# Two transformer layers on one core: who loads first, and which engine does the small casts, sums and block additions

## The chip, the core and the metric

One core of a Trainium2 chip runs the whole program. Its engines work side by side, each through its own queue of instructions in a fixed order: TensorE (PE in the profile; PEld is its weight load), VectorE (DVE), ScalarE (ACT), GpSimd (POOL) and SyncE (SP). An instruction that has to wait holds up all that stand behind it on its engine. The metric is the device time of one execution in microseconds; the kernel before takes 326.74 us, the median of 3 runs (326.48 to 327.2).

## The reference

Two layers over 256 tokens of 1024 features. Everything is float32; the kernel keeps float32 accuracy by splitting each operand of a big product in two.

```python
def even_layer(x, norm_g, w_in, b_f, gn_g, w_out):
    h = rms_norm(x, norm_g)
    q_f, k_f, v_f, f_l, q_r, k_r, v_r, z = jnp.split(h @ w_in, EVEN_SPLITS, axis=-1)
    o_f = fox_attention(q_f, k_f, v_f, f_l + b_f)        # 8 heads, forget gates
    o_r = retention(q_r, k_r, v_r) * gn_g                # 8 heads, group norm
    return x + (concatenate([o_f, o_r]) * silu(z)) @ w_out

def odd_layer(x, ...):
    h = rms_norm(x, norm_g)
    q, kc, vc, ks, vs, kw, vw, gl, z = jnp.split(h @ w_in, ODD_SPLITS, axis=-1)
    k_cmp = silu((blocks of 32 tokens of kc + pe_k) @ wk1) @ wk2      # the same for v_cmp
    o = gated sum of attention to compressed blocks, selected blocks, and a window
    return x + (o * silu(z)) @ w_out

out = rms_norm(odd_layer(even_layer(x)), final_g)
```

## The kernel before, in words

**The stream of big products.** The weights of both layers come as 38 chunks of up to 280 columns (1 MB each). `Feed.load` fetches a chunk into one of three stage buffers `st` (line 148), `Feed.split` cuts it by quarters into `wh` (a copy at the precision of the product, line 95 on ScalarE, line 97 on VectorE) and `wl` (the rest in bf16, line 102 on VectorE), and a chunk feeds two units of 8 steps. A step is three products on TensorE: high by high (lines 194, 214), low by high (195, 215), bf16 by `wl` (196, 216). The next chunk is loaded once a stage buffer is free. The other operand is split the same way, k = 0 to 7 in slices of 128 features: `h` (x0h, x1h, y0h, y1h), `l` (x0l, x1l ..., line 119 or 102) and `b`, the bf16 copy of `h` (x0b, x1b, y0b, y1b; line 99, on GpSimd).

**The first loads.** xT (the input, in four pieces of 256 KB, two slices of k each) and chunk 0 (in_w0v, four pieces of 264 KB) are issued in turn by SyncE, all in one queue, with gv (the factors of the norms) ahead and chunk 1 (two halves), the biases, the constants and chunk 2 behind. Of the slices x0h, ScalarE makes k = 0, 1, 2, 4, 5, 6 and VectorE k = 3 and 7. While the loads are on their way TensorE runs 24 products of zeros (`warm`).

**The norms.** Layer 0 squares xT on ScalarE and adds the eight squares up in a tree of three additions (`sq`, then `acc_n`): the first on VectorE, the others on GpSimd. pc_n and pn_n (lines 257, 248) sum over the partitions on TensorE, and r_n, R_n (243, 244) are the factors; the first values (line 306, 308) leave PSUM with them. The other two norms add one square after the other into `acc_n` on GpSimd (line 240 calls line 102), the last square of the final norm aside.

**The compressed blocks.** After the out projection of layer 0 (products pp_o, additions `xT` at line 381, then x1h, x1l, x1b and the square of each m), `build` takes keys and values kc, vc and writes `ab`: for each of the 4 pairs of kv and u one multiply (line 427) and 8 additions of pe on VectorE. The products `ph` (line 707) take all of ab; TensorE reaches the first of them between two units of pp_ks.

**The order.** The text of the kernel is laid out by a scheduler that fixes the queue of each engine when the program is built; it weighs the loads and operations by its own estimates. So an edit in one place can move instructions in another. The end is the multiply of x2 by R_n in five pieces on VectorE and GpSimd (lines 876 to 880), each followed by its store.

Of the kernel before, what the change touches and what calls it, by code (L numbers as in the profile page):

```python
# [10 lines left out]
F32 = mybir.dt.float32  # L11
# [19 lines left out]
NEARLY = _C["T0"][0]   # columns that layer 0 needs  # L31
# [14 lines left out]
LEAD = 22          # steps by which a chunk of weights is split ahead of its first product  # L46
# engine of each small operation: A scalar, V vector, G gpsimd
E = dict(whi="AAAA", wlo="VVVV", xhi="AAAAAAAA", x0hi="AAAVAAAV", w0hi="AAAV", xb="G", sq="A", acc="G", yhi="A", ylo="G", yb="G", sz="G",
         q2h="AA", q2l="GG", a0="A", a1="V", ac="V", norm="GGGG", pn="G", kh="AA", kl="VV", ab="VVVV", pT="A", cs="GG", tree="VGG", xg="AAAAAAAA")
FIN = (("V", 0, 1), ("G", 1, 1), ("V", 2, 2), ("G", 4, 1), ("V", 5, 3))  # L50
# [3 lines left out]
def trunk_kernel(ctx: ExitStack, tc: tile.TileContext, a: dict):  # L54
# [19 lines left out]

    A.preload_act_table_set("natural_log_exp_and_others")
# [52 lines left out]
    # A chunk is up to 280 columns of a weight matrix: loaded, split into wh (f32r) + wl (bf16), and used by  # L128
    # two units of 8 steps. run(n) issues the next n steps, with the splits and loads that are due.
    class Feed:  # L130
# [11 lines left out]
        def load(s, parts=1, between=None):  # L142
# [4 lines left out]
            for i in range(parts):  # L147
                nc.sync.dma_start(c["st"][:, q * i:q * i + q, :n], c["ap"][:, q * i:q * i + q, :])
                if between:
                    between(i)  # L150
            s.loaded += 1

        def split(s):
            """the next quarter of a chunk"""
# [27 lines left out]
    def mtile(col, xs, kind, name, done):  # L182
        """128 output features as partitions, all tokens; done(psum) after the last step."""
# [18 lines left out]
    def vtile(tt, x, kind, name, done):  # L202
        """128 tokens as partitions, the chunk's columns free."""
# [18 lines left out]
    class Norm:  # L222
        """sum of squares over features -> rsqrt(mean + eps), as [P, S] and as columns."""
# [55 lines left out]
    # ================= layer 0: the stream =================  # L279
# [722 lines left out]
```

## Time and profile before

| | |
|---|---|
| median of 3 runs | 326.74 us |
| span of the profiled execution, first to last instruction | 324.8 us |
| TensorE busy | 307.5 us, 95% of the span |
| VectorE busy | 228.9 us, 70% |
| ScalarE busy | 202.7 us, 62% |
| GpSimd busy | 126.3 us, 39% |
| mean granted TensorE clock | 0.987 of full |
| read from HBM | 48.24 MB |

The runs are timed around the span, and their median stands 1.9 us above it. TensorE is busy for nearly the whole span, so its gaps and its clock are what one looks for first; the shares of the other engines say little, since each is nearly full in some stretches and idle in others.

### The profile page before, as it was taken

How to read it: one execution, taken by the hardware profiler on the slowest of the kernel's cores; microseconds unless marked ns; L12 is line 12 of the kernel's file. 1: busy time of each engine (PE TensorE's matmuls, PEld its weight loads, DVE VectorE, ACT ScalarE, POOL GpSimd, SP SyncE). 2: the span in 40 equal slices, each digit the busy share in tenths (PEclk: the TensorE clock that was granted, in tenths of full speed). 3: DMA queues.
4: the chain of work that ended last, by engine and by line, in shares of the span. 5: the costliest groups of instructions: out<-in, count | busy, mean ns of one | idle time of the engine just before them, and what ended most of it. 6: DMA issues, size and time to landing. Idle time of an engine off the chain costs nothing.

```text
span 324.8 us, 6784 instructions
## 1 busy us (share of the span) xinstructions
PE 307.5 (95%) x2478; PEld 256.4 (79%) x2478; DVE 228.9 (70%) x686; ACT 202.7 (62%) x547; POOL 126.3 (39%) x202
## 2 busy tenths in 40 slices
PE   6879999999999999999987999999999999999990
PEld 4668888888888887888875767898988898888870
DVE  2978964665656656189998856798978798882433
ACT  4749545666645556287622647598988898881461
POOL 2450011541522133375200001267779777973152
PEclk9999999999999999999997999999999999999997
DMA  6995897664155334407717892325421442100003
GB/s 180 363 308 197 264 390 257 227 226 142 59 171 178 132 108 153 129 2 219 244 69 240 281 314 89 127 67 195 131 64 69 133 129 76 56 2 0 3 0 129
DMA packets 43138, 49.72 MB, mean 153 GB/s; under 512 B 1633, under 2 KB 39777, under 8 KB 42849
## 3 DMA queue, kind: packets, MB, share of 16 engines
q1 hardware_dynamic: 42816, 49.03, 45.9%
q8 instruction: 19, 0.31, 0.4%
q10 hardware_dynamic: 288, 0.26, 0.2%
q14 instruction: 15, 0.11, 0.1%
HBM read 48.24 MB, written 1.05 MB: 152 GB/s over the span
## 4 chain that ended last, share of the span: by engine, by line
PE 73%; DVE 16%; ACT 3%; DMA 2%; POOL 2%; issue 1%; SPq 1%; DVEq 0%; ACTq 0%
DVE wl L102 6%; PE pp_q L194 5%; PE pp_z L196 4%; PE pp_q L196 4%; PE pp_z L194 4%; PE pp_z L195 4%; PE pp_q L195 4%; PE pp_o L196 4%; PE po L838 4%; PE pp_o L194 4%; PE pp_o L195 3%; PE ph L707 3%; DVE ab L102 3%; PE pp_k L194 3%; PE pp_k L196 2%; PE pp_k L195 2%
## 5 line engine op out<-in xcount | busy, mean ns | idle before, releaser
L102 DVE TENSOR_TENSOR wl<-st,wh 128x512 bf16<-128x512 f32 (+2 forms) x152 | 108.2, 740 | 13.8 <-ACT wh L95 12.0
L95 ACT ACTIVATE wh<-st 128x512 fp32r<-128x512 f32 (+2 forms) x151 | 87.6, 621 | 43.1 <-PE pp_o L195 8.5
L196 PEld LDWEIGHTS <-wl 128*128 128x128 bf16 x512 | 49.0, 96 | 22.5 <-issue 0.2
L108 POOL TENSOR_SCALAR p<-p,st 128x128 f32<-128x128 f32 (+1 forms) x80 | 42.7, 551 | 51.3 <-DVE st L598 31.9
L782 ACT ACTIVATE p<-ns,st 128x128 f32<-128x128 f32 (+1 forms) x64 | 28.4, 444 | 7.7 <-DVE st L770 6.2
L102 POOL TENSOR_TENSOR q<-q,q 64x256 fp32r<-64x256 f32 x16 | 12.1, 754 | 45.9 <-ACT q L95 44.8
L214 PE MATMUL pp_v<-wh,x0h 128*128 128x256 f32 (+1 forms) x64 | 23.4, 368 | 1.4 <-ACT wh L95 1.4
L194 PE MATMUL pp_o<-y0h,wh 128*128 128x256 f32 x64 | 23.3, 366 | 0.4 <-DVE xT L381 0.4
L194 PE MATMUL pp_q<-x0h,wh 128*128 128x256 f32 x64 | 23.5, 368 | 0.0
L194 PE MATMUL pp_k<-x0h,wh 128*128 128x256 f32 x64 | 23.2, 365 | 0.0
L194 PE MATMUL pp_z<-x0h,wh 128*128 128x256 f32 x64 | 23.2, 365 | 0.0
L194 PE MATMUL pp_o<-y1h,wh 128*128 128x256 f32 x64 | 23.1, 363 | 0.0
L194 PE MATMUL pp_q<-x1h,wh 128*128 128x256 f32 x64 | 22.7, 356 | 0.0
L194 PE MATMUL pp_z<-x1h,wh 128*128 128x256 f32 x64 | 22.6, 355 | 0.0
L770 DVE CUSTOM_DVE_ANT_0 ns<-s,cst 128x128 f32<-128x128 f32 (+1 forms) x64 | 20.1, 350 | 0.0
L216 PE MATMUL pp_v<-wl,x0b 128*128 128x256 bf16 (+1 forms) x64 | 17.9, 283 | 1.1 <-DVE wl L102 1.0
L196 PE MATMUL pp_z<-x0b,wl 128*128 128x256 bf16 x64 | 18.1, 283 | 0.0
L196 PE MATMUL pp_q<-x0b,wl 128*128 128x256 bf16 x64 | 18.1, 283 | 0.0
L196 PE MATMUL pp_o<-y0b,wl 128*128 128x256 bf16 x64 | 18.1, 283 | 0.0
L196 PE MATMUL pp_o<-y1b,wl 128*128 128x256 bf16 x64 | 18.1, 283 | 0.0
L196 PE MATMUL pp_k<-x0b,wl 128*128 128x256 bf16 x64 | 18.1, 283 | 0.0
L196 PE MATMUL pp_q<-x1b,wl 128*128 128x256 bf16 x64 | 18.1, 283 | 0.0
(322 smaller groups left out, 1000.9 us busy)
## 6 DMA issues: line engine op xcount, KB each, us to landing
st<-in_w0c_dram SPq DMA_DIRECT2D x13, 1024.0 KB, 5.8
st<-in_w1c_dram SPq DMA_DIRECT2D x12, 1024.0 KB, 5.6
w<-in_wkv_dram SPq DMA_DIRECT2D x8, 512.0 KB, 4.8
st<-in_w0o_dram SPq DMA_DIRECT2D x4, 1024.0 KB, 5.7
st<-in_w1o_dram SPq DMA_DIRECT2D x4, 1024.0 KB, 5.6
st<-in_w1v_dram SPq DMA_DIRECT2D x2, 1120.0 KB, 5.0
st<-in_w0c_dram SPq DMA_DIRECT2D x4, 512.0 KB, 8.9
dec<-in_dec_dram SPq DMA_DIRECT2D x2, 768.0 KB, 7.7
```

Of the source, the lines that this page charges most:

```text
L95: A.activation(o, x, AF.Copy)
L102: (V if e == "V" else G).tensor_tensor(o, x, y, op=op)
L108: (V if e == "V" else G).tensor_scalar(o, x, c, 1.0, op0=OP.mult, op1=OP.mult)
L194: T.matmul(p, wh[:, k, cs], x.h[:, k], start=(k == 0), stop=False)
L195: T.matmul(p, wh[:, k, cs], x.l[:, k], start=False, stop=False)
L196: T.matmul(p, wl[:, k, cs], x.b[:, k], start=False, stop=(k == KT - 1))
L214: T.matmul(p, x.h[:, k, ts], wh[:, k, :n], start=(k == 0), stop=False)
L216: T.matmul(p, x.b[:, k, ts], wl[:, k, :n], start=False, stop=(k == KT - 1))
L707: T.matmul(ph[64 * kv:64 * kv + 64, :256], ab[:, kv, 2 * qr + j].rearrange("p g c -> p (g c)"), w1[qr][:, kv, j], start=(qr == 0 and j == ...
L770: V.tensor_tensor_reduce(out=out, in0=pp[:, lo:lo + n], in1=C(tab, lo, lo + n), scale=-slope, scalar=3e38, op0=OP.add, op1=OP.min, accum_o ...
L782: A.activation(p[:, d:d + n], ns[:, d:d + n], AF.Exp, scale=-1.0, bias=st[:, qt, br, 0:1], accum_out=st[:, qt, br, 1:2])
L838: T.matmul(po[64 * j:64 * j + 64, 256 - n:256], vs[:, kt, vc:vc + 64], m[:, br * n:br * n + n], start=False, stop=(br == 1 and kt == 1))
```

## The change

- gv is issued by GpSimd's queue, xT by SyncE's, chunk 0 by ScalarE's, ahead of its table load. Chunks 1 and 2 follow on SyncE.
- The bf16 copies `b` (x0b, y0b, x1b, y1b: 32 casts), the sums `acc_n` of the norms (13 additions) and the tree of layer 0 (2 additions) run on VectorE.
- `build` writes ab in 4 additions of 64 x 240 elements per call where it took 8 of 64 x 120.
- The last multiply is three pieces (3, 3 and 2 slices), all on VectorE.

```diff
-E = dict(... xb="G", sq="A", acc="G", yhi="A", ylo="G", yb="G", sz="G",
-         ... cs="GG", tree="VGG", xg="AAAAAAAA")
-FIN = (("V", 0, 1), ("G", 1, 1), ("V", 2, 2), ("G", 4, 1), ("V", 5, 3))
+E = dict(... xb="V", sq="A", acc="V", yhi="A", ylo="G", yb="V", sz="G",
+         ... cs="GG", tree="VVV", xg="AAAAAAAA")
+FIN = (("V", 0, 3), ("V", 3, 3), ("V", 6, 2))
...
-        kc4 = kc.rearrange("p (b j r) -> p b j r", j=8, r=2)
         for gi in range(2):
             gr = slice(64 * gi, 64 * gi + 64)
             for par in range(2):
-                for jh in range(2):
-                    binary(E["ab"][2 * gi + par],
-                           ab[64 * par:64 * par + 64, kv, 8 * jh:8 * jh + 8, 2 * u + gi, 0:15],
-                           kc4[gr, jh:jh + 15, :, par].rearrange("p c j -> p j c"),
-                           pe[gr, kv, par, 8 * jh:8 * jh + 8].unsqueeze(2).to_broadcast([64, 8, 15]), OP.add)
+                o = ab[64 * par:64 * par + 64, kv, :, 2 * u + gi, 0:15].rearrange("p (h j) c -> p h j c", h=2)
+                x = bass.AP(kc.tensor, kc[gr, par:par + 1].offset, [list(kc[gr].ap[0]), [16, 2], [2, 8], [16, 15]])
+                y = pe[gr, kv, par].rearrange("p (h j) -> p h j", h=2).unsqueeze(3).to_broadcast([64, 2, 8, 15])
+                binary(E["ab"][2 * gi + par], o, x, y, OP.add)
...
-    nc.sync.dma_start(gv, a["gv"])
...
-    nc.sync.dma_start(xT[:, 0:2], a["xT"][:, 0:2])
-    def more(i):
-        if i < 3:
-            nc.sync.dma_start(xT[:, 2 * i + 2:2 * i + 4], a["xT"][:, 2 * i + 2:2 * i + 4])
-    feed.load(4, more)
+    nc.gpsimd.dma_start(gv, a["gv"])
+    for i in range(4):
+        nc.sync.dma_start(xT[:, 2 * i:2 * i + 2], a["xT"][:, 2 * i:2 * i + 2])
+    feed.load(4, nc.scalar)
+    A.preload_act_table_set("natural_log_exp_and_others")
     feed.load(2)
```

**First place: VectorE's queue at the start.** x0h, x0l and x0b are slices of 128 x 256; what an instruction waits for stands in brackets. Before (DMAHW1, 3, 5 and 7 are the four pieces of xT, 2 and 4 pieces of chunk 0):

```order
L119 SCALAR_TENSOR_TENSOR x0l<-xT,gv,x0h 128x256 [waits DMAHW1_49,DMAHW0_49,Activation_49]
L119 SCALAR_TENSOR_TENSOR x0l<-xT,gv,x0h 128x256 [waits Activation_49]
L108 TENSOR_SCALAR x0h<-xT,gv 128x256 [waits DMAHW3_49]
L102 TENSOR_TENSOR wl_170<-st_147,wh_169 128x2x264 [waits DMAHW2_49,Activation_49]
L119 SCALAR_TENSOR_TENSOR x0l<-xT,gv,x0h 128x256 [waits Activation_49]
L119 SCALAR_TENSOR_TENSOR x0l<-xT,gv,x0h 128x256 [waits DVE_49]
L102 TENSOR_TENSOR wl_170<-st_147,wh_169 128x2x264 [waits DMAHW4_49,Activation_49]
```

The same place now, where DMAHW1, 2, 4 and 6 are the four pieces of xT in their order, DMASW0 is gv, and DMAHW0 is the first piece of chunk 0:

```order
L106 TENSOR_SCALAR x0h<-xT,gv 128x256 [waits DMAHW2_49,DMASW0_49]
L117 SCALAR_TENSOR_TENSOR x0l<-xT,gv,x0h 128x256 [waits DVE_49]
L95 CAST x0b<-x0h 128x256
L106 TENSOR_SCALAR x0h<-xT,gv 128x256 [waits DMAHW6_49]
L117 SCALAR_TENSOR_TENSOR x0l<-xT,gv,x0h 128x256 [waits DMAHW1_49,Activation_49]
L95 CAST x0b<-x0h 128x256
L117 SCALAR_TENSOR_TENSOR x0l<-xT,gv,x0h 128x256 [waits Activation_49]
L95 CAST x0b<-x0h 128x256
L100 TENSOR_TENSOR wl_170<-st_149,wh_169 128x2x264 [waits DMAHW0_49,Activation_49]
```

VectorE's own two slices (k = 3, from the second piece, and k = 7, from the last) have moved ahead of x0l of k = 0, and each x0l is followed by its cast.

**Second place: VectorE's queue at the end of layer 0's out projection and in `build`.** Before, around the additions of m = 4 and 5 and the first blocks:

```order
L381 TENSOR_TENSOR xT<-pp_o_4_1825,xT 128x256 [waits PE_49]
L102 TENSOR_TENSOR wl_1776<-st_1580,wh_1775 128x2x256 [waits Activation_49] x2
L119 SCALAR_TENSOR_TENSOR x1l<-xT,gv,x1h 128x256 [waits Activation_49]
L102 TENSOR_TENSOR wl_1871<-st_1677,wh_1870 128x2x256 [waits DMAHW1_49,Activation_49]
L102 TENSOR_TENSOR wl_1871<-st_1677,wh_1870 128x2x256 [waits Activation_49]
L381 TENSOR_TENSOR xT<-pp_o_5_1863,xT 128x256 [waits PE_49]
...
L427 TENSOR_TENSOR kc_2055<-pp_kc_1981,R_n_2045 128x256 [waits Activation_49]
L427 TENSOR_TENSOR kc_2065<-pp_kc_2009,R_n_2045 128x256
L102 TENSOR_TENSOR ab<-kc_2055,pe 64x8x15 [waits DVE_49]
L102 TENSOR_TENSOR ab<-kc_2055,pe 64x8x15 x7
```

The same rows now:

```order
L377 TENSOR_TENSOR xT<-pp_o_4_1825,xT 128x256 [waits PE_49]
L100 TENSOR_TENSOR wl_1871<-st_1677,wh_1870 128x2x256 [waits DMAHW0_49]
L100 TENSOR_TENSOR wl_1871<-st_1677,wh_1870 128x2x256
L117 SCALAR_TENSOR_TENSOR x1l<-xT,gv,x1h 128x256 [waits Activation_49]
L95 CAST x1b<-x1h 128x256
L100 TENSOR_TENSOR acc_n_96<-acc_n_96,sq_n_1860 128x256 [waits Activation_49]
L377 TENSOR_TENSOR xT<-pp_o_5_1863,xT 128x256 [waits PE_49]
...
L423 TENSOR_TENSOR kc_2055<-pp_kc_1981,R_n_2045 128x256 [waits Activation_49]
L423 TENSOR_TENSOR kc_2061<-pp_kc_2009,R_n_2045 128x256
L100 TENSOR_TENSOR ab<-kc_2055,pe 64x16x15 [waits DVE_49]
L100 TENSOR_TENSOR ab<-kc_2055,pe 64x16x15 x3
```

Between two additions of xT there are now a cast and a sum more, and a block takes 4 additions in place of 8.

## Rows read from the trace of the kernel before

**Rows 1.** Waits of TensorE: us in total, times, longest.

```profile
PE ph L707 <- DVE ab L102: 3.1, 1, 3.1
PE pc_n L257 <- POOL acc_n L102: 1.9, 1, 1.9
PE pp_v L214 <- ACT wh L95: 1.4, 1, 1.4
...
PE pp_o L194 <- DVE xT L381: 0.4, 1, 0.4
```

**Rows 2.** Windows: us; busy PE, PEld, DVE, ACT, POOL; PEclk, DMA share, GB/s.

```profile
19.50:20.50 1.00, 0.00 (x0) 0.00 (x0) 1.00 (x2) 0.06 (x1) 0.92 (x2) 1.00 1.03 312
...
139.00:158.00 19.00, 18.56 (x153) 16.17 (x153) 19.00 (x31) 14.55 (x32) 12.01 (x15) 1.00 0.45 140
...
173.00:202.00 29.00, 29.00 (x217) 20.82 (x213) 20.67 (x45) 17.24 (x41) 0.52 (x1) 0.94 0.72 243
```

**Rows 3.** Chain that ended last, first 21 us: start, us, what.

```profile
4.36 0.85 SPq L539
5.26 7.23 DMA st<-in_w0v_dram
...
15.57 4.07 POOL sq L102
...
20.81 0.61 PE pc_n L257 x4
```

**Rows 4.** Tile xT in the first 20 us: ns, and time to landing.

```profile
L119 DVE SCALAR_TENSOR_TENSOR x0l<-xT,gv,x0h x8: 476/612/620, 6.2 to 13.3; 128x256 fp32r<-128x256 f32 x8
...
DMA to landing us min/median/max: 4.4/5.5/6.6
```

**Rows 5.** Timeline of VectorE at the start: start us, us, what.

```profile
12.86 0.87 DVE L119 SCALAR_TENSOR_TENSOR x0l<-xT,gv,x0h 128x256 fp32r<-128x256 f32 x2
...
14.27 1.22 DVE L102 TENSOR_TENSOR sq<-sq 128x1024 f32<-128x1024 f32 x1
...
24.32 0.57 DVE L308 SCALAR_TENSOR_TENSOR fl<-pp_v,r_n,bias 128x8 f32<-128x8 f32 x2
```

**Rows 6.** Timeline of TensorE: two steps of chunk 2, and ph.

```profile
24.61 0.37 PE L214 MATMUL pp_v<-wh,x0h 128*128 128x256 f32 x1
...
24.98 0.36 PE L214 MATMUL pp_v<-wh,x0h 128*128 128x256 f32 x1
...
172.59 1.78 PE L707 MATMUL ph<-w,ab 128*64 128x256 f32 x10 [3.08 <-DVE ab L102]
```

**Rows 7.** Timeline of VectorE, out projection of layer 0 to the blocks.

```profile
138.88 1.15 DVE L381 TENSOR_TENSOR xT<-pp_o,xT 128x256 f32<-128x256 f32 x3 [4.55 <-PE pp_o L196]
...
147.39 1.28 DVE L102 TENSOR_TENSOR wl<-st,wh 128x512 bf16<-128x512 f32 x2
...
150.66 1.22 DVE L102 TENSOR_TENSOR wl<-st,wh 128x512 bf16<-128x512 f32 x1
...
160.05 0.74 DVE L427 TENSOR_TENSOR kc<-pp_kc,R_n 128x256 f32<-128x256 f32 x2
160.72 5.13 DVE L102 TENSOR_TENSOR ab<-kc,pe 64x120 f32<-64x120 f32 x16
```

**Rows 8.** Groups of VectorE by shape: count, busy us, mean ns.

```profile
L102 DVE TENSOR_TENSOR ab<-kc,pe 64x120 f32<-64x120 f32 x32 | 9.9, 350 | 0.2
L102 DVE TENSOR_TENSOR KL<-kf,KH 64x256 fp32r<-64x256 f32 x16 | 6.7, 418 | 0.5 <-ACT KH L95 0.3
...
L102 DVE TENSOR_TENSOR KL<-kcf,KH 64x16 fp32r<-64x16 f32 x8 | 1.4, 172 | 0.2
...
L336 DVE CAST sel<-cst 104x1024 fp32r<-104x1024 f32 x1 | 0.7, 682 | 0.0
```

**Rows 9.** Timeline of the last multiply.

```profile
318.28 2.95 DVE L102 TENSOR_TENSOR xT<-xT,R_n 128x256 f32<-128x256 f32 x3 [2.25 <-ACT R_n L244]
318.32 2.09 POOL L102 TENSOR_TENSOR xT<-xT,R_n 128x256 f32<-128x256 f32 x2 [3.80 <-ACT R_n L244]
```

More of the change, by code (lines that the diff above doesn't have):

```diff
@@ L46 @@
 LEAD = 22
-E = dict(whi="AAAA", wlo="VVVV", xhi="AAAAAAAA", x0hi="AAAVAAAV", w0hi="AAAV", xb="G", sq="A", acc="G", yhi="A", ylo="G", yb="G", sz="G",
-         q2h="AA", q2l="GG", a0="A", a1="V", ac="V", norm="GGGG", pn="G", kh="AA", kl="VV", ab="VVVV", pT="A", cs="GG", tree="VGG", xg="AAAAAAAA")
-FIN = (("V", 0, 1), ("G", 1, 1), ("V", 2, 2), ("G", 4, 1), ("V", 5, 3))
+E = dict(whi="AAAA", wlo="VVVV", xhi="AAAAAAAA", x0hi="AAAVAAAV", w0hi="AAAV", xb="V", sq="A", acc="V", yhi="A", ylo="G", yb="V", sz="G",
+         q2h="AA", q2l="GG", a0="A", a1="V", ac="V", norm="GGGG", pn="G", kh="AA", kl="VV", ab="VVVV", pT="A", cs="GG", tree="VVV", xg="AAAAAAAA")
+FIN = (("V", 0, 3), ("V", 3, 3), ("V", 6, 2))
 @with_exitstack
@@ L73, in bank @@
         return pool.tile([P, 512], F32, tag=tag, name=name)
-    A.preload_act_table_set("natural_log_exp_and_others")
     xT = cp.tile([P, KT, S], F32, name="xT")
@@ L140, in chunk, with load @@
                 s.steps.append(lambda f=fns[i], k=k: f(k))
-        def load(s, parts=1, between=None):
+        def load(s, parts=1, queue=nc.sync):
             c = s.chunks[s.loaded]
@@ L147, in load @@
             for i in range(parts):
-                nc.sync.dma_start(c["st"][:, q * i:q * i + q, :n], c["ap"][:, q * i:q * i + q, :])
-                if between:
-                    between(i)
+                queue.dma_start(c["st"][:, q * i:q * i + q, :n], c["ap"][:, q * i:q * i + q, :])
             s.loaded += 1
```

## The prediction

> **What bounds the kernel now.** I read first who waits for whom on TensorE, since it is busy for 95% of the span: each gap in it is time, and work on another engine counts only where it makes or closes one. There are three gaps worth naming [rows 1]: 3.1 us before ph, which waits for the blocks ab; 1.9 us before pc_n, for the sum of squares acc_n; 1.4 us before the first product. The windows [rows 2] add the clock. In the stretch from 173 to 202 us, which begins with the gap before ph, the mean granted clock is 0.94: 6% of 29 us at full speed is 1.7 us of TensorE's work lost, since the clock stood at its lower level, 1.2 GHz, for some 3.5 us. So the gap before ph costs 3.1 + 1.7 = 4.8 us. The wait for acc_n, 1.9 us long, left the clock at 1.00 [rows 2]: here 1.9 us of idleness did no harm to it and 3.1 us did.
>
> The timeline of VectorE [rows 7] says why ph waits. From 138.88 us VectorE goes without a pause: additions, splits and low parts until 160.05, then the blocks until ab is whole and ph goes on at 172.59 [rows 6]. In the window from 139 to 158 it is busy 19.00 of 19 us [rows 2], with TensorE at 18.56. So here, and only here, VectorE sets the pace; from 173 us to the end of the last product TensorE does, and work given to VectorE there lies under it.
>
> **The change part by part.** *VectorE from 138.88 to 160.05, 21.17 us.* Here stand 18 splits wl, 8 additions xT, 8 low parts x1l. Beside a silent GpSimd two wl take 1.28 us, some 0.60 apiece with the small overlap; one alongside a GpSimd operation takes 1.22 [rows 7]. Of x0l two take 0.87, 0.435 apiece, against a median of 0.61 for one [rows 5, 4]. Three additions take 1.15, some 0.35 apiece with overlap [rows 7]. Undisturbed: 18 x 0.60 + 8 x 0.35 + 8 x 0.435 = 17.1 us. So about 4 us of the 21.17 is VectorE and GpSimd slowing each other, and with the casts and sums gone from GpSimd it goes. What comes is 8 casts x1b and 7 sums. No row has this cast; the nearest is sel, 1024 elements in 0.682 us [rows 8], so 256 lie between a quarter of that, 0.17, and the 0.42 of a two-operand operation of 256 [rows 8]; I take 0.25, near the sel row, which is a copy too: 2.0 us (1.4 to 3.4). The sums are like KL, 0.418, or 0.35 with overlap: 2.45. Together 17.1 + 2.0 + 2.45 = 21.55 us, 0.4 more than now (-0.2 to +1.8): here the extra work is paid for by the peace. The blocks begin at about 160.45.
>
> *The blocks.* 16 additions of 120 elements take 5.13 us, 0.32 apiece [rows 7]; two of them are now one of 240. KL gives 172 ns for 16 elements and 418 for 256 [rows 8], that is 156 ns plus 1.025 per element. By this line 120 elements would take 279, yet ab shows 350 [rows 8]: 71 more, for its short strided runs. If that grows with the runs, 240 elements take 156 + 246 + 142 = 544 ns, 0.51 with the overlap; if it is paid once, 0.44 with it. No row shows the new form: the ends are 0.40 (the plain line) and 0.64 (nothing saved). I take 0.50, next to what growing runs give. Then from 160.45: two kc 0.67, 16 x 0.50 = 8.0, two more kc 0.7, two wl 1.2: ab is whole at 171.0 (169.4 to 173.2).
>
> *The gap before ph.* TensorE comes to it at 172.59 - 3.08 = 169.5 [rows 6]; I take 169.7, since some units of pp_o now wait a little longer for the later additions xT. The gap falls to 1.3 us, under the 1.9 that left the clock alone. ph starts 1.6 us sooner and the 1.7 of the clock are kept: -3.3 us. At the ends: ab at 169.4 closes the gap, -2.7 - 1.7 = -4.4; ab at 173.2 leaves it and the slow clock, +0.6.
>
> *The start.* In the order of VectorE's queue its x0h of k = 7 stands before x0l of k = 0, and it waits for the last piece of xT. TensorE's second product needs x0l of k = 0, so beyond its first product TensorE stands until then; queued behind the wait on VectorE are all the low parts and casts of x0 but k = 3's, and the wl of chunks 0 to 2. Before, the last piece was issued at 4.36 [rows 3] and landed 6.6 us later [rows 4], at 10.96; the last of chunk 0 landed at 5.26 + 7.23 = 12.5 [rows 3]. Now all eight are in flight from two queues, half a microsecond sooner. If the last of xT is as the last of eight, it lands at 12.0; if xT's pieces of 256 KB get ahead of the weights it may come by 8.4, 2.5 us sooner than now. I take 10.2, the middle.
>
> The Trainium skill (DMA: Bandwidth & Descriptors, "Issuing engines are not separate DMA queues") says that loads issued from several engines run on the same DMA engines and that only issue time is saved. The DMA share of 1.03 at 312 GB/s [rows 2] is of that kind: these engines are full while the loads come. By the rule alone the last of xT would land at 10.5 or later, against 10.2, and the sum would be 0.3 higher.
>
> From that landing VectorE has, in order: x0h 0.35, 7 x0l 3.05, 7 x0b 1.75, wh 0.35, and 5 wl of which the last is the last quarter of chunk 0: 3.1; that is 8.6 us. Then 3 wl, the tree's 1024 elements in 1.14 [rows 5], wl, 512 in 0.6, wl, 256 in 0.35: 5.1, and acc_n is there at 10.2 + 13.7 = 23.9, against 20.8 now [rows 3], though GpSimd's 4.07 and 1.06 us are gone. Then two wl, sel and the first fl (0.25, half the pair of 0.57 [rows 5]), 2.05 us, and chunk 2 may start, as its PSUM bank is held until fl has read it: 25.95 us. Before, chunk 2 starts at 24.61 [rows 6]. So the start loses 1.35 us (-0.45 at 8.4, +3.15 at 12.0). TensorE itself keeps up: 96 products of chunks 0 and 1 at 0.12 us, three to a step of 0.37 [rows 6], are 11.5 us, and half of them can run as VectorE feeds them. Its 4 us of idleness before may drop its clock as at ph; in the 3.5 us that this lasted there it falls behind by 1.7 us, about what it has spare (8.6 us for 50 products of 0.12, 6.0 us). gv on GpSimd's queue has no row; between nothing and the 4.4 us that a piece of xT takes [rows 4] it still comes before the slice that VectorE waits for. The table load behind four issues on ScalarE, and a decay table that is now issued ahead of chunk 3, lie under the same wait and under 5.8 us of TensorE's work per chunk.
>
> *The rest.* y0b and y1b, 16 casts, are 4 us on VectorE where TensorE sets the pace: nothing, with as their cover the slack of VectorE there; the waits for y1h that they bring hold up its queue by little (price up to 0.5 us). The last sums: nothing, VectorE idles between the last additions.
>
> *The end.* Now the three pieces on VectorE take 2.95 us beside GpSimd's 2.09 [rows 9]. By the 1024 elements in 1.22 [rows 5], undisturbed pieces of 768, 768 and 512 take 0.87 + 0.87 + 0.69 = 2.4. The last store starts 0.5 us sooner, but the first, of three slices, starts 0.5 later; I take -0.4 (-0.9 to -0.1).
>
> **Sum.** +1.35 - 3.3 - 0.4 = -2.35: the span of 324.8 becomes 322.45. The median of the runs lies 1.94 above the span (326.74), and I let that stand: 324.4 us.
>
> **The rivals.** *Slower: the new additions cost as two.* At 0.64 apiece ab is whole at 173.2, the gap is 3.5 us and the clock falls as before: 326.74 + 1.35 + 0.6 - 0.4 = 328.3. For it: the 71 ns that short runs already cost; against it: the 156 ns fixed that KL shows. It decides at the gap at which the clock falls, between 1.9 and 3.1 us; ab whole at 171.6 to 172.8, so 0.54 to 0.61 apiece. *The start is starved and the clock stays low.* TensorE gets its products by handfuls until about 19 us; if the clock is at 1.2 GHz until then, 50 products take 12 us in place of 8.6, and the start loses 3.4 more: 327.8. For it: the gap is longer than that before ph; against it: there the clock came back while TensorE worked. *The queues do what they are named for.* If the last of xT lands by 8.4 the start gains 0.45 in place of losing 1.35: 322.6. For it: eight issues need 2 us in place of 5; against it: a full DMA. *Nothing much:* the gap at ph stays at 2 us, the clock holds by half, the start loses 2.5: about 326.5.
>
> **How the numbers follow.** Forecast 50%, 323.2 to 325.9. New additions as two 13%, low clock at the start 12%, gain at the start 15%, nothing much 10%. A measurement of this kernel can tell about 0.2%, 0.65 us, from no change. Faster by more: the forecast (0.49) and the gain (0.15), 0.64. Within it: "nothing much" and a share of the two slow ones, 0.14. Slower: the rest of these, 0.22. The range, from the gain at the start to the slow cases but for their ends: 322.2 to 328.0.
>
> **What would show it.** Right: a gap before ph under 2 us and a clock of 1.00 from 173 to 202; ab at about 0.5 us each; wl at 0.6 throughout 139 to 158; TensorE idle after its first product until about 11 us, its next wait ended by x0l; chunk 2 starting near 26. Wrong: casts at 0.4 or sums at 0.7 between 139 and 158, a clock below 1.00 there or in the first 20 us, or the first low part made before 9 us.

## The result, and the profile after

The changed kernel takes 334.45 us (median of 4 runs, 333.28 to 334.76) against 326.61 us: a ratio of 1.0239 (95% interval 1.0205 to 1.0273), 2.4% slower, 7.8 us. The prediction said 324.4 us, at most 328.0. The profiled execution has a span of 333.0 us (324.8 before) and a mean granted clock of 0.972 (0.987).

Waits of TensorE after (us in total, times, longest):

```profile
PE pp_v L210 <- ACT wh L93: 4.6, 1, 4.6
PE ph L698 <- DVE ab L100: 2.9, 1, 2.9
PE po L821 <- DVE ac L816: 2.5, 7, 0.7
...
PE pp_v L211 <- DVE x0l L117: 0.6, 1, 0.6
...
PE s L750 <- POOL q L100: 0.4, 1, 0.4
```

Against [rows 1]: the wait for acc_n is gone, the one before ph is as long as it was (2.9 for 3.1), the one before the first product has grown from 1.4 to 4.6, and one is new, seven times, 2.5 us: po, the output of the sparse attention, waits for ac (the transposed attention weights of the compressed blocks, copied by VectorE out of PSUM, where the products are written).

How far the profile after lags behind the one before, at the same instruction: first product of chunk 2 +3.1 us (27.74 for 24.61), first kc +2.9, ph +2.2 (174.76 for 172.59), first po of the sparse attention +4.6 (229.38 for 224.81), its last +8.1, end of the span +8.2. So 3 us are lost at the start, one is won back on the way to ph, 2.4 go between ph and po, and 3.5 in the eight tiles of the sparse attention (a tile is two heads; its period is the time from po to the next po), where the prediction looked for nothing.

The start, on ScalarE and VectorE (start us, us, what; in brackets the idle time before and what ended it):

```profile
8.38 0.91 ACT L104 ACTIVATE x0h<-xT,gv 128x256 fp32r<-128x256 f32 x2 [3.81 <-DMA gv<-in_gv_dram]
```

```profile
8.38 0.35 DVE L106 TENSOR_SCALAR x0h<-xT,gv 128x256 fp32r<-128x256 f32 x1 [7.10 <-DMA gv<-in_gv_dram]
...
10.25 0.35 DVE L106 TENSOR_SCALAR x0h<-xT,gv 128x256 fp32r<-128x256 f32 x1 [0.79 <-DMA xT<-in_xT_dram]
```

gv, 14 KB, issued at 1.27, lets its readers go at 8.38. The last piece of xT is there at 10.25, where the prediction had 10.2. The windows after (us; busy PE, PEld, DVE, ACT, POOL; clock; DMA share, GB/s):

```profile
8.00:12.00 4.00, 1.54 (x4) 1.13 (x5) 2.79 (x9) 3.62 (x9) 0.00 (x0) 0.50 1.05 356
12.00:16.00 4.00, 3.61 (x17) 2.99 (x16) 4.00 (x12) 3.68 (x8) 0.00 (x0) 0.50 1.01 368
16.00:20.00 4.00, 4.00 (x29) 3.63 (x27) 4.00 (x10) 3.45 (x7) 0.00 (x0) 0.79 0.71 269
...
142.00:161.00 19.00, 18.63 (x154) 16.31 (x154) 18.95 (x46) 14.50 (x33) 0.00 (x0) 1.00 0.44 134
176.00:205.00 29.00, 29.00 (x216) 20.62 (x214) 18.63 (x42) 15.89 (x39) 0.00 (x0) 0.96 0.72 232
```

Having stood still from 5.3 to 9.9 us, TensorE makes its first products at 1.2 GHz. From 142 to 161 GpSimd is silent, as intended, with VectorE as full as before [rows 2].

VectorE after, in that stretch, in the blocks, and at the last multiply:

```profile
144.09 0.29 DVE L95 CAST x1b<-x1h 128x256 bf16<-128x256 f32 x1
...
144.89 0.42 DVE L100 TENSOR_TENSOR acc_n<-acc_n,sq_n 128x256 f32<-128x256 f32 x1
...
147.10 1.28 DVE L100 TENSOR_TENSOR wl<-st,wh 128x512 bf16<-128x512 f32 x2
...
162.93 0.76 DVE L423 TENSOR_TENSOR kc<-pp_kc,R_n 128x256 f32<-128x256 f32 x2
163.61 4.65 DVE L100 TENSOR_TENSOR ab<-kc,pe 64x240 f32<-64x240 f32 x8
...
172.47 2.24 DVE L100 TENSOR_TENSOR ab<-kc,pe 64x240 f32<-64x240 f32 x4
```

```profile
326.30 2.43 DVE L100 TENSOR_TENSOR xT<-xT,R_n 128x768 f32<-128x768 f32 x3 [2.19 <-ACT R_n L240]
```

From the first addition xT (142.03) to kc (162.93) VectorE takes 20.90 us; 21.55 was forecast, 21.17 it took before [rows 7]. The new additions to ab take 0.56 to 0.58 us apiece in their row (4 in 2.24 us, 8 in 4.65); 0.50 was forecast.

### The profile page after: what moved, and what is told of

Its sections match the earlier page's. It is cut to its first block, busy times and chain, and to the rows that moved or that the text cites. A ratio compares the mean times of both kernels' runs of the same rounds, so it can differ in the third digit from the quotient of the medians.

```text
span 333.0 us, 6748 instructions
## 1 busy us (share of the span) xinstructions
PE 311.2 (93%) x2478; PEld 258.5 (78%) x2478; DVE 235.5 (71%) x717; ACT 202.5 (61%) x547; POOL 90.9 (27%) x154
## 4 chain that ended last, share of the span: by engine, by line
PE 68%; DVE 18%; ACT 8%; DMA 3%; issue 2%; DVEq 0%; POOL 0%; POOLq 0%; ACTq 0%
DVE wl L100 5%; ACT p L773 5%; PE pp_q L190 4%; PE pp_q L192 4%; PE pp_o L192 4%; PE pp_o L190 4%; PE pp_q L191 4%; PE pp_o L191 3%; PE pp_v L212 3%; PE pp_v L210 3%; PE pp_v L211 3%; PE po L829 3%; PE ph L698 3%; DVE ab L100 2%; PE pp_k L190 2%; PE pp_z L192 2%
## 5 line engine op out<-in xcount | busy, mean ns | idle before, releaser
L100 DVE TENSOR_TENSOR wl<-st,wh 128x512 bf16<-128x512 f32 (+2 forms) x152 | 103.8, 713 | 6.3 <-ACT wh L93 4.5
L210 PE MATMUL pp_v<-wh,x0h 128*128 128x256 f32 (+1 forms) x64 | 24.7, 390 | 5.3 <-ACT wh L93 4.6
L190 PE MATMUL pp_o<-y0h,wh 128*128 128x256 f32 x64 | 23.3, 366 | 0.4 <-DVE xT L377 0.4
L211 PE MATMUL pp_v<-wh,x0l 128*128 128x256 f32 (+1 forms) x64 | 19.2, 304 | 0.6 <-DVE x0l L117 0.6
L210 PEld LDWEIGHTS pp_v<-wh,x0h 128*128 128x128 f32 x64 | 14.1, 221 | 6.0 <-ACT wh L93 4.8
```

The costliest lines, as they stand in the source:

```text
L100: (V if e == "V" else G).tensor_tensor(o, x, y, op=op)
L190: T.matmul(p, wh[:, k, cs], x.h[:, k], start=(k == 0), stop=False)
L210: T.matmul(p, x.h[:, k, ts], wh[:, k, :n], start=(k == 0), stop=False)
L211: T.matmul(p, x.l[:, k, ts], wh[:, k, :n], start=False, stop=False)
```

## The experiments: the four parts alone

Ratios are to the kernel before on the same chip, with their 95% intervals; 0.1% is 0.33 us.

**First loads alone.** Chunk 0 on ScalarE's queue, xT on SyncE's, gv on GpSimd's, the table load behind.

```diff
-    A.preload_act_table_set("natural_log_exp_and_others")
...
-    nc.sync.dma_start(gv, a["gv"])
-    (xT and chunk 0 in turn on nc.sync)
+    nc.gpsimd.dma_start(gv, a["gv"])
+    (xT on nc.sync)
+    feed.load(4, nc.scalar)
+    A.preload_act_table_set("natural_log_exp_and_others")
```

> The kernel before with the first loads from three queues and nothing else of the change. Theory: in the trace of after the start is 3.1 us late (sr at 93.32 for 90.18) because gv, issued at 1.27, lets its readers go only at 8.38; that belongs to the loads alone. So here the scaled slices start near 8.4, TensorE's first product is near 9.9, chunk 2 starts near 27.7 for 24.61, and the time is 3.1 us over before, near 329.7 (1.0095), with the period of a tile of the sparse attention at 10.8 us as before. Rival 1 (the loads set off all of it, the later losses being the clock's answer to the late start): 333 or more. Rival 2 (the late start is the casts' and the sums' on VectorE): within 1 us of before, chunk 2 near 25.

Measured: 331.27 us, 1.0157 (1.0094 to 1.0219), so 5.1 us. The scaled slices start at 7.97, behind gv, and the clock is 0.50 from 12 to 16 us; the period of a tile stays at 10.8. Rival 2 falls, and the later losses of rival 1 don't show. The loads do cost the start, and about two us more than the forecast from the trace of after, though the interval still holds that forecast (1.0095): TensorE waits 2.0 us for acc_n here, whose tree still runs on GpSimd, where in the changed kernel it waits for none of it, and the first product sr of the retention comes 4.4 us later than before (94.55 for 90.11), against 3.1 in the changed kernel.

**Casts and sums alone.**

```diff
-xb="G" ... acc="G" ... yb="G" ... tree="VGG"
+xb="V" ... acc="V" ... yb="V" ... tree="VVV"
```

> The kernel before with the casts to bf16 and the sums of the norms on VectorE and nothing else of the change. Theory: these cost the 3.5 to 4 us that after loses between 225 and 305, where a tile of the sparse attention takes 11.36 us for 10.82; the start stays as it is. So the time is near 330.5 (1.012), first product of the last tiles +4, and TensorE waits for the products ac with the pairs again (seven waits, some 2.5 us, in after). Rival 1 (the late start causes all): within 1 us of before, the period 10.8. Rival 2 (the larger additions, which leave less of VectorE free, cause it): the same.

Measured: 328.79 us, 1.0077 (1.0045 to 1.011). po follows po at 11.37 us for 10.82, with seven waits for ac, 2.4 us; the first product sr of the retention comes at 88.30, for 90.11 before and 89.16 in the profile of the last multiply alone. Both rivals fall; the sum is 2.5 us and not 4, since some of the loss is won back ahead of sr.

**The larger additions alone.**

```diff
-for jh in range(2): binary(..., 64 x 8 x 15)
+binary(..., 64 x 16 x 15)
```

> The kernel before with the 16 additions of 64x240 for 32 of 64x120 and nothing else of the change. Theory: the gap before ph goes from 3.08 to near 2.0 us, as sixteen additions of 0.57 us end some 1 us earlier than thirty-two of 0.35 (pitch 0.30 or so); so the time is 325.5, 1 us faster (0.997). Rival: the gap stays at 2.9 as in after, and the time is that of before within 0.4 us.

Measured: 327.99 us, 1.0072 (1.0033 to 1.011): a part that has less work is slower. Neither theory had that. The tile ab and the waits of TensorE in this run:

```profile
L102 DVE TENSOR_TENSOR ab<-kc,pe x16: 547/562/579, 159.9 to 170.4; 64x240 f32<-64x240 f32 x16
```

```profile
PE ph L706 <- DVE ab L102: 3.1, 1, 3.1
...
PE ph L706 <- DMA w<-in_wkv_dram: 0.9, 1, 0.9
```

From kc until ph goes on it is 11.8 us for 12.5 (159.23 to 171.06; 160.05 to 172.59 before): 0.7 is won, and the wait for it is as long as ever. The reason stands in the order of TensorE's queue, here counted in rows from the program's start:

```
before                          additions halved
1586 MATMUL ph                  1586 MATMUL ph
1599 MATMUL ph x3  <- the wait  1591 MATMUL ph x3  <- the wait
1600 MATMUL ph x4               1600 MATMUL ph x4
1646 MATMUL ph x4               1638 MATMUL ph x4
```

The scheduler knows that the additions are shorter and puts the waiting products two steps (0.36 us each) earlier, and later groups of ph as well. The 0.9 us of waiting for w are another thing: that transfer takes 6.8 us here (issued at 180.30), where its counterpart before took 4.9 (issued at 181.49); why isn't shown, and the changed kernel has no such wait. From pth, the first product that needs what ph made, to the first exponential p it is 8.4 us for 7.0 (200.21 to 208.60, and 199.73 to 206.77 before). The order is different there too: on ScalarE the eight copies KH now stand ahead of the pair q that the first scores need, and on VectorE a wl stands ahead of the scores; which of them makes the 1.4 us isn't separated.

**The last multiply alone.**

```diff
-FIN = (("V", 0, 1), ("G", 1, 1), ("V", 2, 2), ("G", 4, 1), ("V", 5, 3))
+FIN = (("V", 0, 3), ("V", 3, 3), ("V", 6, 2))
```

> The kernel before with the last multiply in three pieces on VectorE and nothing else of the change. Theory: the tail behind the last product is some 0.1 us longer or the same, as in after; the time is that of before within 0.5 us. Rival (the prediction's own term): 0.4 us faster, 326.2.

Measured: 326.01 us, 0.9998 (0.9964 to 1.0033). Nothing.

## The experiments: which casts

**y0b and y1b alone** (TensorE's order is that of before, row for row).

```diff
-yb="G"
+yb="V"
```

> The kernel before with the sixteen casts y0b and y1b alone on VectorE; the products stand in TensorE's order as before. Theory: y1b stands in VectorE's queue between the weight remainders and the scores of the next pair, waits there for ScalarE's y1h and then for GpSimd's running instruction (0.63 us instead of 0.29), so scores, exponentials and ac come 0.55 us later in every tile: the period of the sparse attention is 11.37 us for 10.82, TensorE waits seven times for ac, and the time is some 4 us over before, 330.3 (1.012). Rival (the loss comes from all 32 casts and 13 sums together, which fill VectorE): a period under 11.0 and less than 2 us over before.

Measured: 329.79 us, 1.0112 (1.0064 to 1.016), period 11.38. VectorE, GpSimd and TensorE in one tile of this run:

```profile
240.23 0.65 DVE L102 TENSOR_TENSOR wl<-st,wh 128x512 bf16<-128x512 f32 x1
241.02 0.63 DVE L97 CAST y1b<-y1h 128x256 bf16<-128x256 f32 x1
241.57 0.41 DVE L97 COPY a<-ptB 128x256 f32<-128x256 f32 x1
...
242.19 0.16 DVE L770 CUSTOM_DVE_ANT_0 nsc<-s,cst 128x16 f32<-128x16 f32 x1
```

```profile
240.76 0.74 POOL L102 TENSOR_TENSOR sz(1, 2)_3108<-sz(1, 2)_3108,z(1, 2)_3106 128x256 f32<-128x256 f32 x1 [0.53 <-ACT sz(1, 2)_3108 L265]
```

```profile
236.28 0.38 PE L830 MATMUL po<-ac,zch 64*128 64x256 f32 x1 [0.32 <-DVE ac L825]
...
247.66 0.38 PE L830 MATMUL po<-ac,zch 64*128 64x256 f32 x1 [0.31 <-DVE ac L825]
```

From wl to the scores nsc VectorE takes 1.96 us; without y1b in between it was 1.21 (239.40 to 240.61). Of the 0.75 us, 0.14 is a pause before the cast, 0.55 the cast until the next one starts. The rival falls. VectorE has no slack in this piece of the loop: scores, exponentials on ScalarE, weights, ac, po follow one another, and TensorE's order had just filled the time (po after po at 10.82 us with no wait listed but the first). The windows of the tiles, before and here (columns as above):

```profile
225.00:290.00 65.00, 65.00 (x555) 56.20 (x555) 54.96 (x253) 55.80 (x184) 51.08 (x92) 1.00 0.26 82
```

```profile
225.00:290.00 65.00, 63.42 (x532) 54.13 (x532) 54.06 (x240) 51.83 (x171) 46.19 (x80) 1.00 0.25 82
```

TensorE is idle 0.3 us of each tile in front of po. The rest of the 0.55 doesn't show as idle time: it counts as busy for 63.42 of 65 us and yet gets through 532 products for 555. Five of the seven periods are 0.55 us longer, one 0.8, the last none. All of it is y1b's: with y0b on VectorE kc comes at 159.25, against 159.10 and 159.28 with it on GpSimd and the same order of TensorE (the last multiply alone, gv alone), so the eight y0b cost nothing that shows.

**x0b, x1b, the sums and the tree alone.**

```diff
-xb="G" ... acc="G" ... tree="VGG"
+xb="V" ... acc="V" ... tree="VVV"
```

> The kernel before with the casts x0b and x1b, the sums of the norms and the tree on VectorE, y casts on GpSimd as before. Theory: the wait of 1.9 us for acc_n goes and nothing is lost in the sparse attention (period 10.82), so the time is 1.3 us below before, 325.0 (0.996). Rival (all casts cost alike): period 11.1 or more, 328 or more.

Measured: 325.52 us, 0.9987 (0.9956 to 1.0018); period 10.82, pc_n at 19.95. The sign is as expected, the size a third of it and within the measurement. The rival falls.

**The changed kernel with the y casts back on GpSimd.**

```diff
-yb="V"
+yb="G"
```

> The changed kernel with the casts y0b and y1b back on GpSimd and nothing else undone. Theory: the period of a tile of the sparse attention returns to 10.82, and 4 us of the 7.8 come back: 330.4 (1.012 of before). Rival (the later losses are the clock's, set off by the start): within 1 us of the changed kernel, 333.5 or more.

Measured: 330.46 us, 1.0151 (1.0091 to 1.0211) of before; the period is 10.82 again. The rival falls. The y casts are 2.9 us of the changed kernel's loss when they are taken out (1.0239 to 1.0151), 3.6 when they are put in alone.

**Why y1b takes 0.63 us.** The y casts on VectorE, and GpSimd's two operations around them too.

```diff
-yb="G" ... ylo="G" ... sz="G"
+yb="V" ... ylo="V" ... sz="V"
```

> The kernel before with the y casts on VectorE, as in y_casts_only, and with the multiplies sz and the low parts y1l and y0l on VectorE too, so that GpSimd runs nothing around y1b. Only the length of y1b is asked for. Theory: in y_casts_only most of the y1b took 0.63 us where x0b and x1b took 0.29, because a GpSimd operation on two operands was running when they began and they were held until it ended; with GpSimd silent there, y1b takes 0.29. Rival (the 0.63 comes of the wait for ScalarE's y1h or of something else in this stretch): still 0.6. The time itself is 6 us or more over before, since VectorE has 16 low parts and 16 multiplies more.

The tile y1b in this run, and in y_casts_only (ns, minimum, median, maximum):

```profile
L97 DVE CAST y1b<-y1h x8: 280/285/286, 230.8 to 306.9; 128x256 bf16<-128x256 f32 x8
```

```profile
L97 DVE CAST y1b<-y1h x8: 295/631/857, 229.6 to 305.2; 128x256 bf16<-128x256 f32 x8
```

So a GpSimd operation under way is what makes a cast of 0.29 us one of 0.63: in the tile above the cast ends (241.65) 0.15 us after GpSimd's sz (241.50). The sixteen casts y0b and y1b of y_casts_only all fit: the nine that start beside a GpSimd operation end 0.15 us behind it, or behind the next one that follows it at once (0.46 to 0.86 us long), and the seven where GpSimd's starts 0.01 to 0.05 us after them take 0.29. The Trainium skill (SBUF — State Buffer, "SBUF: two separate sides") says that VectorE and GpSimd share a pair of ports: a VectorE operation in a two-port mode (or with two inputs in SBUF, where GpSimd's reads SBUF) and a GpSimd operation lock it for a whole instruction, so that the one that comes second waits. These rows agree.

The hold isn't the whole price, though. With the low part, the cast and the multiply all on VectorE, wl to nsc is 2.08 us and the period 11.48 (1.96 and 11.38 in y_casts_only, 1.21 and 10.82 before): the period goes with the length of this piece. The time of the one run is 331.64 us; what eight casts of 0.29 alone would cost isn't shown.

## The experiments: ph held in its place

**ph three and six steps later, nothing else.** HW is the table of steps between the groups of ph.

```diff
-HW = (40, 3, 3, 3, 3, 3, 3, 3, 3)
+HW = (46, 3, 3, 3, 3, 3, 3, 0, 0)
```

> The kernel before, additions and all, with the first two groups of ph placed three and six steps later in TensorE's order (the first number of the table HW 46 for 40). Theory: the gap before ph is the distance between the place in TensorE's order and the end of the additions; three steps of 0.36 us more before the first whole group shrink it from 3.1 to 2.2 us, and the time by 0.7 to 1 us, to 325.5 (0.997). Rival (what follows waits for the same end of the additions and the w transfers behind it anyway): the gap shrinks and the time stays.

Measured: 325.81 us, 0.9978 (0.9951 to 1.0006): the forecast's size, and not beyond the measurement. The gap is 2.2 us, but 1.9 us are waited for w now. Theory and rival differ by less than the measurement can tell.

**The larger additions with that table.**

```diff
-HW = (40, 3, 3, 3, 3, 3, 3, 3, 3)
+HW = (46, 3, 3, 3, 3, 3, 3, 0, 0)
-for jh in range(2): binary(..., 64 x 8 x 15)
+binary(..., 64 x 16 x 15)
```

> The sixteen larger additions, with ph placed where the run before this one has it. In the changed kernel the planner moved ph forward with the shorter additions, so the gap stayed near 3 us. Theory: with ph held in place the shorter additions show: gap 1.5 us, 0.7 us less than the run before this one, and the time 1.4 us under before, 325.0 (0.996). Rival (the additions gain nothing on the chip): gap and time as in the run before this one or worse.

Measured: 324.66 us, 0.9953 (0.9921 to 0.9984), the gap 1.5 us, as expected. The same additions that cost 0.7% in the scheduler's place for ph are part of a gain of 0.5% with ph held back. Against the run before this one the intervals overlap; the medians, ten runs each on the same chip, are 1.15 us apart (325.81 and 324.66), and the gap is 0.7 us shorter, as the theory has it. Waits and window of this run, and the same window of the additions alone:

```profile
PE ph L706 <- DMA w<-in_wkv_dram: 2.0, 2, 1.8
...
PE ph L706 <- DVE ab L102: 1.5, 1, 1.5
```

```profile
170.00:180.00 10.00, 8.79 (x64) 5.76 (x65) 9.85 (x20) 5.63 (x12) 0.00 (x0) 1.00 0.79 267
```

```profile
170.00:180.00 10.00, 8.94 (x56) 6.00 (x56) 7.86 (x16) 4.02 (x10) 0.00 (x0) 0.83 0.73 247
```

The columns are those of the windows above. TensorE is busy about as long in both, with 64 products in the one and 56 in the other: the clock is 1.00 and 0.83. But the gap doesn't settle the clock by itself. In the last multiply alone, with a gap of 3.1 us and TensorE's order as before, it stays at 1.00 in the same window:

```profile
170.00:180.00 10.00, 8.35 (x64) 6.12 (x66) 9.83 (x23) 5.51 (x12) 0.00 (x0) 1.00 0.76 258
```

There, and in gv alone, it is 25.5 and 25.6 us from ph to pth, for 27.1 before: the price of 1.7 us that the prediction put on the clock is about right, but it isn't paid in every execution. And in the run of this section the clock falls later, behind the wait of 1.8 us for w:

```profile
185.52 1.74 PE L706 MATMUL ph<-w,ab 128*64 128x256 f32 x8 [1.80 <-DMA w<-in_wkv_dram]
```

```profile
186.00:189.00 3.00, 3.00 (x15) 1.48 (x14) 1.76 (x3) 0.72 (x2) 0.00 (x0) 0.50 0.59 184
```

**ph ten steps later.**

```diff
-HW = (40, 3, 3, 3, 3, 3, 3, 3, 3)
+HW = (50, 2, 2, 2, 2, 2, 2, 2, 0)
```

> The kernel before with ph ten steps later in TensorE's order (HW begins with 50, the later groups two or three steps later as well, the products with pth two). Theory: the gap shrinks to 1 us or less, the clock holds 1.00 in 173 to 202, and the time falls by 2 us, 324.5 (0.993). Rival (the work behind ph, hid, pth, the compressed keys and scores, then ends later and TensorE waits there): the time of before or more, with new waits between 195 and 215.

Measured: 325.32 us, 0.997 (0.9945 to 0.9995). The gap is 0.8 us, but the waits for w are 2.9: half of the expected gain, the rest turned into another wait. The clock doesn't hold either: it is 0.92 from 181 to 203, behind a wait of 2.0 us for w. Between 195 and 225 no wait is listed, so the rival is wrong about the place.

## The experiments: the start

**gv from GpSimd's queue alone.**

```diff
-    nc.sync.dma_start(gv, a["gv"])
+    nc.gpsimd.dma_start(gv, a["gv"])
```

> The kernel before with gv issued from GpSimd's queue and nothing else changed; xT is then the first transfer of SP. Theory (transfers land in the order of their issue, whichever queue): gv, issued at 1.27, lands behind the one or two pieces issued before it, at 5.5 to 6.5, so the first scaled slice comes within 1 us of the 5.63 of before, and the time is 0 to 1 us over before. Rival (GpSimd's queue itself takes 7 us for a small transfer): the first scaled slice near 8.4, and 2.5 us or more over before, 329.

Measured: 325.11 us, 0.9997 (0.9954 to 1.0041). Tile gv here, and in the changed kernel: when it is issued, and the time to its landing.

```profile
L527 POOL DMA_DIRECT2D gv<-in_gv_dram x1: 730/730/730, 1.3 to 1.3; - x1
...
DMA to landing us min/median/max: 4.6/4.6/4.6
```

```profile
L528 POOL DMA_DIRECT2D gv<-in_gv_dram x1: 727/727/727, 1.3 to 1.3; - x1
...
DMA to landing us min/median/max: 7.1/7.1/7.1
```

The same queue, the same moment of issue, 2.5 us apart. By 1.3 us two pieces of 256 KB had been issued ahead of it here and four in the changed kernel; in both gv lands 0.2 us behind the last of them. The rival (the queue itself is slow) falls: the theory's 5.5 to 6.5 us for the landing holds (5.91). The Trainium skill (DMA: Bandwidth & Descriptors, "Queues, rings and completion order") says that the signal of a finished transfer comes only after all earlier writes of its DMA engine, whichever queue they are from; the two landings agree with it.

**The changed kernel with gv first on SyncE's queue.**

```diff
-    nc.gpsimd.dma_start(gv, a["gv"])
+    nc.sync.dma_start(gv, a["gv"])
```

> The changed kernel with the scales gv back as the first transfer of SP's queue, ahead of xT; the weights stay on ScalarE's queue. Theory: gv's landing behind the big transfers was what held the start; its readers now go when the first pieces of xT land, near 5.3, the last slice stays at 10.2, chunk 2 starts near 26 for 27.7, the clock holds 1.00 from 8 to 18, and the time is 1.7 to 3 us below the changed kernel, 331.5 to 332.8. Rival (the weights on ScalarE's queue share the engines with xT and hold both): no gain, 334 or more, the first scaled slice still near 8.

Measured: 335.51 us, 1.0301 (1.0244 to 1.0358). gv lands 2.0 us after its issue, and the kernel is not faster but has the highest ratio of all. The theory as put falls, and the rival has the time right, but not for its reason. VectorE and TensorE in this run:

```profile
9.11 0.29 DVE L95 CAST x0b<-x0h 128x256 bf16<-128x256 f32 x1
11.31 0.43 DVE L95 CAST wh<-st 128x528 fp32r<-128x528 f32 x1 [1.92 <-DMA st<-in_w0v_dram]
11.66 0.48 DVE L117 SCALAR_TENSOR_TENSOR x0l<-xT,gv,x0h 128x256 fp32r<-128x256 f32 x1
```

```profile
8.18 0.39 PE L210 MATMUL pp_v<-wh,x0h 128*128 128x264 f32 x1 [2.37 <-ACT wh L93]
12.19 0.59 PE L211 MATMUL pp_v<-wh,x0l 128*128 128x264 f32 x1 [3.62 <-DVE x0l L117]
```

The scheduler has put the cast of the last quarter of chunk 0, the last piece to land, ahead of x0l of k = 0, whose data came with the first piece of xT (ScalarE's first x0h starts at 6.68). TensorE waits 3.6 us for a remainder that could have been made four us before.

**The same, with VectorE's x0h and wh on ScalarE.**

```diff
-x0hi="AAAVAAAV", w0hi="AAAV"
+x0hi="AAAAAAAA", w0hi="AAAA"
```

> The changed kernel with gv first on SP's queue, as in the run after_gv_first, and besides with the two scaled slices and the last quarter of the first weights that VectorE makes there on ScalarE instead. In after_gv_first VectorE's queue held a cast of the last weight quarter (landed 11.29) ahead of the remainders x0l of slices that had long landed, and TensorE waited 3.6 us for one. Theory (the start is held by VectorE's order and by gv's place, not by the landing times, whose last is 11.3 for 12.5 before): no wait over 1.5 us for x0l, chunk 2 starts near 25.5 and the time is 2 us under the changed kernel, 332.5. Rival (the shared transfer engines hold all the pieces, so that the order doesn't matter): 334 or more, chunk 2 at 27.5 or later.

Start of TensorE in this run:

```profile
7.69 0.59 PE L210 MATMUL pp_v<-wh,x0h 128*128 128x264 f32 x1 [2.29 <-ACT wh L93]
...
24.27 0.35 PE L210 MATMUL pp_v<-wh,x0h 128*128 128x256 f32 x1 [1.81 <-DVE fl L304]
```

No wait for x0l is left, and chunk 2 starts at 24.27 for 27.74, before even [rows 6]. So VectorE's order and gv's place held the start, not the shared engines. Yet the time is 333.57 us, 1.0227 (1.0186 to 1.0269): at the first product sr of the retention 1.9 of the 3.5 us are left (91.31 for 93.25), as the clock stands at 0.59 from 24 to 28 us behind the wait of 1.8 for fl, and at the first po 0.8; the clock from 170 to 180 is 0.66 here and 0.83 in the changed kernel. The time that the theory asked for (332.5) isn't reached. The start is explained; that the whole gain there arrives at the end isn't shown.

**The changed kernel with the old first loads.**

```diff
-    nc.gpsimd.dma_start(gv, a["gv"])
-    (xT on nc.sync)
-    feed.load(4, nc.scalar)
+    nc.sync.dma_start(gv, a["gv"])
+    (xT and chunk 0 in turn on nc.sync)
```

> The changed kernel with the first loads undone: one queue, gv first, weights between the pieces of xT, the table load ahead. Theory: the start's 3.1 us come back and the rest of the loss stays (y casts 3.6, the additions' order 1 to 2): 331.0 (1.014). Rival (the parts add up as they were measured alone, 5.0 for the loads): 329.5.

Measured: 330.15 us, 1.015 (1.011 to 1.019), the theory's figure within the measurement: undone, the loads give back some 3 us, and alone they cost 5.1 (3.1 at the lower end of the interval). The parts alone add up to 10.6 us (5.1 - 0.4 + 3.6 + 2.4 - 0.1, each from its ratio), the whole is 7.8; the intervals, each about 1 us or more either way, leave open whether that is more than their error.

**What gained or cost nothing, together.** From before: x casts, sums and tree on VectorE, the larger additions, the table HW with 46, the last multiply on VectorE; y casts and first loads as before.

```diff
-xb="G" ... acc="G" ... tree="VGG"
+xb="V" ... acc="V" ... tree="VVV"
-HW = (40, 3, 3, 3, 3, 3, 3, 3, 3)
+HW = (46, 3, 3, 3, 3, 3, 3, 0, 0)
 (the additions and FIN of the change)
```

> The kernel before with what gained or cost nothing alone: x casts, sums and tree on VectorE, the sixteen larger additions with ph held later (HW begins with 46), the last multiply on VectorE; the y casts and the first loads as before. Theory: the parts add up, 0.4 and 1.5 us, 324.5 (0.994 of before). Rival (both fill the same slack of VectorE): 325.5 or more.

Measured: 323.47 us, 0.9932 (0.9901 to 0.9962), 0.7% faster than before, as the theory has it. Its waits:

```profile
PE ph L706 <- DVE ab L102: 1.5, 1, 1.5
PE ph L706 <- DMA w<-in_wkv_dram: 1.3, 1, 1.3
```

## Why the prediction was wrong, by its steps

**VectorE from 138.88 to kc: right.** 20.90 us for the forecast 21.55. wl is 0.60 beside a silent GpSimd as said (two in 1.28); behind a cast the next operation starts 0.20 us after it for the 0.25 taken, behind a sum 0.34 for 0.35. The extra work there was paid for by the peace.

**The blocks: the size was off, by the rival's measure.** 0.57 us apiece where the step took 0.50; the rival "the new additions cost as two" had its bounds at 0.54 to 0.61. The regular cost of short runs does grow with the runs: 562 ns in the additions alone, against the 544 of that reading.

**The gap before ph: a step that wasn't looked at.** 3.3 us were to be gained from an end of the blocks at 171.0 against a TensorE that comes at 169.7 "since some units of pp_o now wait a little longer". With the 2.9 us that kc lags taken off, ph goes on at 171.9, 0.7 us sooner than before and not 1.6, and TensorE comes at 168.9, 0.6 sooner than before: the scheduler moved ph forward. The order of the changed kernel showed that, and the prediction gave the place in TensorE's order as fixed. Gap 2.9 us, clock 0.83 in 170 to 180, nothing gained; with the place held, the same additions do gain (additions_halved_ph_back). Behind ph the new order costs more: of the 2.4 us lost between ph and po, 1.4 stand between pth and the first exponential, 8.4 us as in the additions alone (202.90 to 211.31), where it is 7.0 before and with ph held back. The changed kernel with ph held back wasn't run.

**The clock behind that gap: the price right, its condition not.** The prediction read from one profile that 1.9 us of idleness do no harm and 3.1 do. Other profiles have 1.00 behind 3.1 us, and a fall to 0.50 behind 1.8.

**The start: VectorE's chain right, TensorE's backlog wrong.** xT's last piece came at 10.25 for 10.2; 10.2 was the middle between two bounds, so the hit is luck. VectorE's queue from there was priced well: acc_n is whole at 23.3 for 23.9. But pc_n, which reads it, starts at 25.51, and without a wait:

```profile
22.87 0.42 DVE L100 TENSOR_TENSOR acc_n<-sq 128x256 f32<-128x256 f32 x1
```

```profile
25.51 0.50 PE L253 MATMUL pc_n<-ones,acc_n 128*128 128x1 f32 x4
```

The step that failed is "TensorE itself keeps up". Its first product came at 9.88, its idleness ran to 4.6 us, the clock was 0.50 from 8 to 16 and 0.79 from 16 to 20, and from 16 to 26 it worked without a pause at what it was behind with. The 23 products from 12.47 to 17.62 took 0.22 us apiece; at 0.12 they would have taken up to 2.4 us less (an estimate from these rows), about the 2.2 that pc_n comes behind acc_n. That is the rival "the start is starved and the clock stays low", which had 12%. One of its causes is gv, which was to land "between nothing and the 4.4 us that a piece of xT takes" and took 7.1. It did come before the slice that VectorE waits for (8.36 against 10.25), but the step asked only for VectorE: ScalarE needs gv too, for k = 0 and 1, and its first slice came at 8.38 for the 5.63 of before. The other cause is a VectorE that waits for a late piece ahead of x0l of k = 0: with gv early and such a wait left, the clock is still 0.56 and 0.50 from 8 to 16 (after_gv_first); with neither, it is 1.00 from 12 to 24 (after_gv_first_all_scalar). Chunk 2 starts 3.1 us late, inside the term's bounds (-0.45 to +3.15) but at their far end.

**The rest: the step that failed with the most at stake.** The 16 casts y0b and y1b stood at "nothing, with as their cover the slack of VectorE there", at a price of up to 0.5 us. y_casts_only: +3.6 us, and none of it by y0b. VectorE's busy share in the sparse attention is below full and TensorE's was 65.00 of 65 us, so TensorE seemed to set the pace alone. But VectorE's free time lies elsewhere in the tile; between wl and the scores it stands in the loop, where each y1b costs 0.55 us of the period in five of seven, partly because GpSimd holds it.

**The end: 2.4 us as forecast, and no gain.** The three pieces take 2.43 us for 2.95, but from the last product of the out projection to the end of the span it is 0.1 us longer. The last store is issued 0.5 us sooner after the first multiply (2.5 us behind it for 3.0), as forecast, and lands 3.0 us after its issue in place of 2.5; that this comes of the stores standing closer together is argued, not shown. The term was -0.4; alone it measures 0.9998.

In place of +1.35 - 3.3 - 0.4 + 0, the trace shows +3.1 at the start, -0.2 for VectorE's stretch and -0.7 for the blocks up to ph, +2.4 from ph to po, +3.5 in the tiles and +0.1 at the end: 8.2. The sum of the rivals was never priced: each stood alone, while here two came together with a step that had no rival. Two side sums don't come out either, and neither touches the forecast: with ab whole at 169.4 the gap's end gains 2.9 us (172.59 to 169.7) and not 2.7, and the terms of "nothing much" make 327.1 and not 326.5.

## What to carry to other kernels

Where a scheduler sets the order, a shorter operation moves its readers forward with it: read where the waiting instruction stands in its queue after the edit, and hold it in place if the gap is to close. "Engine X has slack in this stretch" is no cover for an operation inside a loop: look at what stands right behind it in the queue, and who waits for that. A small load that everything needs goes out ahead of the big ones, and an instruction that waits for the last piece must not stand early in a queue: here only the two together brought the start back.

## What the runs showed of the hardware

- Landing follows the order of issue across queues to within about 0.2 us: gv landed 2.0 us after its issue with nothing issued ahead of it, 4.6 behind two pieces of 256 KB, 7.1 behind four. It isn't strict: in after_gv_first the last piece of xT, issued 1.4 us after the last of chunk 0 (3.71 and 2.27), landed 0.2 us ahead of it (11.10 and 11.29). No run issues gv at the same place from two engines, so the engine's own part isn't measured.
- A cast of 128 x 256 to bf16 on VectorE takes 0.29 us, and 0.46 to 0.86 (mostly 0.63) when a GpSimd operation is running as it starts; it then ends 0.15 us behind GpSimd. A GpSimd operation that starts 0.01 us later no longer holds it.
- TensorE's clock and gaps: where TensorE stood still for 2.8 to 3.1 us before ph, the window from 170 to 180 shows a clock of 0.66 to 0.89 in twelve profiles and 1.00 in two (the last multiply alone, gv alone); with 2.2, 1.5 and 0.8 us it was 1.00 in all four, but in two of these it fell later, behind waits of 1.8 and 2.0 us for w (0.92 from 181 to 203). 1.9 us before pc_n left it at 1.00 in the kernel before.
- An addition of 64 x 240 in runs of 15 takes 562 ns (64 x 120 took 350), against the 418 of a plain one with 256 elements [rows 8].
